# Up projection of a two-layer decoder trunk: high and low halves of the activations taken in one 512-column product

## The chip, the cores and the metric

The kernel runs on 1 core of one Trainium2 chip. The metric is the device time of one execution in microseconds, the median of several runs. Engines are named as in the profile: PE (TensorE, with PEld for its weight loads), DVE (VectorE), ACT (ScalarE), POOL (GpSimd) and SP (SyncE, which here only issues loads).

## The reference, cut to what matters

Two layers run one after the other on 256 rows of 1024 channels. Each has a mixer (two attention branches, gates, an output projection), a feed-forward part with a causal convolution, and a gated embedding. The change lies in the feed-forward part:

```python
def conv_ffn(u, w_up, conv_w, conv_b, w_down):      # u (1, 256, 1024), w_up (1024, 5632)
    up = u @ w_up
    pad = jnp.pad(up, ((0, 0), (CONV_W - 1, 0), (0, 0)))            # CONV_W = 3
    conv = conv_b + sum(pad[:, j:j + length] * conv_w[j] for j in range(CONV_W))
    gate, val = jnp.split(conv, 2, axis=-1)         # 2816 channels each
    return (jax.nn.gelu(gate, approximate=True) * val) @ w_down
```

All inputs and the output are float32.

## The kernel before, in words

**Three products for one.** A float32 product a·w is made of three products in PE's float32r format. Each operand is split into a high part (rounded to that format) and a low part (what the rounding left), and hi·hi + lo·hi + hi·lo are added up in PSUM.

**Weights.** All weights come as 128 chunks of 128x1024 per layer, in the order of use. `dma_next` (L146) issues a chunk's load on SP into one of 5 `raw` buffers. `split_hi` (L154) makes its high part `wh` on ACT (L159), `split_lo` (L163) its low part `wl` on DVE (L166); after it the next load is issued into the raw buffer that this frees. `chunk` (L195) hands a pair to the products. `tick` (L200), called between pieces of work, goes on with the splitting. In the steady part of the up projection the tick behind chunk n issues the low part of chunk n+4 and then the high part of chunk n+5, so a high part is made one chunk before its low part is asked for, and a low part is issued three chunks before PE reaches it. There are 7 `wh` and 7 `wl` buffers.

**Order.** The order of each engine's instructions is the order in which the program issues them: every engine works through its own queue in order. `Side` (L60) keeps a rough account of the engines' time and decides where side threads (attention pieces, transposes) are put between the products.

**Activations.** `HL` (L271) holds a transposed activation as high tiles and low tiles of 4 k-blocks each, one k-block being 128 channels by 256 rows. `split_T2` (L284) and `ffn_T` (L761) fill it from transposes in PSUM: ACT writes the high part, DVE the low part.

**Up projection (L793 to L825).** A layer has 44 chunks (54 to 97): for each of 22 blocks of 128 channels one chunk of the gate half and one of the value half. For one chunk PE makes 24 products of 256 columns into half of a PSUM bank: for each of 8 k-blocks wh with u's high part (L802), wh with u's low part (L803), wl with u's high part (L804). Then ACT scales the result by the convolution's last tap and adds the bias (L807), and DVE adds the two shifted taps (L809, twice). After each pair ACT makes the gelu (L815) and DVE the product of the halves (L816); the split of that product for the next stage (L821 on ACT, L822 on DVE) is a side thread. Four PSUM banks (`tp`) are used in turn. The down projection (L847) follows, with 22 chunks and 264 products of 512 columns.

**POOL** does small row statistics (L248, L249, L263 to L265) and nothing in the up projection.

Of the kernel before, what the change touches and what calls it, by code (L numbers as in the profile page):

```python
# [9 lines left out]
F32 = mybir.dt.float32  # L10
# [7 lines left out]
P = 128  # L18
# [35 lines left out]
MID_0 = 2  # L54
MID_M = 2
MID_P = 2
NONE = (0.0, 0.0, 0.0)


# [49 lines left out]
def decoder_kernel(ctx: ExitStack, tc: tile.TileContext, x, pT, ws, fc, tb, gf, rope, out):  # L109
# [36 lines left out]
    def dma_next(step=CW):  # L146
# [4 lines left out]
        raws[nx["dma"]] = raw  # L151
        nx["dma"] += 1

    def split_hi():  # L154
        raw = raws[nx["hi"]]
        wh = wpool.tile([P, CW], F32R, name="wh", bufs=SPLITS)
        wl = wpool.tile([P, CW], F32R, name="wl", bufs=SPLITS)
        parts[nx["hi"]] = (wh, wl)
        nc.scalar.activation(wh, raw, AF.Copy)  # L159
        side.work(act=0.95)  # L160
        nx["hi"] += 1

    def split_lo():  # L163
        raw = raws.pop(nx["lo"])
        wh, wl = parts[nx["lo"]]
        nc.vector.tensor_sub(wl, raw, wh.bitcast(F32))  # L166
        side.work(dve=1.12)
        nx["lo"] += 1
        if nx["dma"] < NALL:
            dma_next()  # L170
# [100 lines left out]
    class HL:  # L271


        def __init__(self, name, n=2):
            self.h = [b4(name + "h", F32R) for _ in range(n)]
            self.l = [b4(name + "l", F32R) for _ in range(n)]

        def hi(self, k):
            return self.h[k // 4][:, k % 4, :]

        def lo(self, k):
            return self.l[k // 4][:, k % 4, :]

    def split_T2(srcs, hf, k0, scale, x, between=None):  # L284


        hi, lo = x.h[hf][:, k0:k0 + 2, :], x.l[hf][:, k0:k0 + 2, :]
        n = 1 if callable(scale) else 2
        pts = []
        for a in range(0, 2, n):  # L290
            pt = ps_tp.tile([P, 2, L], F32, name="tp")[:, :n, :]
            pts.append(pt)
            for j in range(n):
                for i in range(2):
                    c = (k0 + a + j) * P
                    nc.tensor.transpose(pt[:, j, i * P:(i + 1) * P], srcs[i][:, c:c + P], ident)  # L296
        for a in range(0, 2, n):
            s = scale if n == 2 else scale(4 * hf + k0 + a)
            nc.scalar.activation(hi[:, a:a + n, :], pts[a], AF.Copy, scale=s)
            nc.vector.scalar_tensor_tensor(lo[:, a:a + n, :], pts[a], s, hi[:, a:a + n, :].bitcast(F32),  # L300
                                           op0=ALU.mult, op1=ALU.subtract)
            if between:
                between(a)
# [119 lines left out]
    for l in range(DEPTH):  # L423
# [238 lines left out]
        def mixer_a(hq, i):  # L662
            while not {"qa", "mask"} <= flags:
                yield NONE
            pe, sums = maps("qa", product_a, i, hq, mask[i])
            yield 0.9 + 0.9 * i, 0.8 + 0.6 * i, MA + MB * i
            rcp = sm.tile([P, 2, 2], F32, name="rcp", bufs=4)
            nc.vector.reciprocal(rcp, sums)
            for hh in range(4):
                nc.vector.tensor_scalar(pe[:, hh, :], pe[:, hh, :], rcp[:, hh % 2, hh // 2:hh // 2 + 1], None,  # L670
                                        op0=ALU.mult)
            yield 0.0, 0.9 + 0.3 * i, 0.0
            pt = ptrans(pe, 4, i)
            yield 0.5 + 0.5 * i, 0.0, 0.5 + 0.5 * i
            nb = i + 1
            ptv = pt[:, :4 * nb, :].rearrange("p (m r s) t -> p m r s t", r=2, s=nb)
            po = ps_tp.tile([P, 2, L], F32, name="tp")[:, 0, :].rearrange("p (m t) -> p m t", t=P)
            for sb in range(nb):
                for r in range(2):
                    nc.tensor.matmul(po[r * 64:(r + 1) * 64], va[:, sb, :], ptv[:, :, r, sb, :],  # L680
                                     start=sb == 0, stop=sb == i)
            x = o_parts()
            hi, lo = (t[0][:, 2 * hq:2 * hq + 2, i * P:(i + 1) * P] for t in (x.h, x.l))
            nc.scalar.activation(hi, po, AF.Copy)
            nc.vector.tensor_sub(lo, po, hi.bitcast(F32))
            yield 0.85 * nb, 0.4, 0.35
            flags.add(("a", hq, i))
# [54 lines left out]
            gemm_a(o["x"], range(4), stream(l, C_BR + 4 + 2 * hf), 512, ev_a)  # L742
        side.until(lambda: "m0" in flags)
        ss = new_ss()
        pxs = HL("px", 1)
        u = HL("u")
        gb = blk.tile([P, D], F32, tag="blk", name="gb")
        nc.scalar.dma_start(gb, gf[l])
# [12 lines left out]
        def ffn_T(i, hf):  # L761
            pt = ps_tp.tile([P, 4, P], F32, name="tp")
            for k in range(4):
                nc.tensor.transpose(pt[:, k, :], un[i][:, hf, k * P:(k + 1) * P], ident)
            hi, lo = (t[hf][:, :, i * P:(i + 1) * P] for t in (u.h, u.l))
            nc.scalar.activation(hi, pt, AF.Copy)
            nc.vector.tensor_sub(lo, pt, hi.bitcast(F32))

        for hf in range(2):
            def ev(i, acc):  # L770
                nc.vector.tensor_add(h[:, i, HALF[hf]], h[:, i, HALF[hf]], acc)

            def mid_m():
                split_T(msrc[1], 1, 0.5, m)
            if hf:
                nc.scalar.activation(pxs.h[0][:, 0:2, :], px, AF.Copy)
                nc.vector.tensor_sub(pxs.l[0][:, 0:2, :], px, pxs.h[0][:, 0:2, :].bitcast(F32))
                gemm_a(m, range(KD), stream(l, C_OUT + 4), 512, ev_n, {13: lambda: ffn_T(0, 0)}, outer=KD)
            else:
                gemm_a(m, range(KD), stream(l, C_OUT), 512, ev, {MID_M: mid_m})  # L780
                sq_half(ss, 0)
# [9 lines left out]


        gx = []  # L793
        for fb in range(NF):
            cc = []
            for s in range(2):
                wh, wl = chunk(l, C_UP + 2 * fb + s)
                wh = wh.rearrange("p (k f) -> p k f", f=P)
                wl = wl.rearrange("p (k f) -> p k f", f=P)
                pu = ps_tp.tile([P, 512], F32, name="tp")[:, :L]  # L800
                for k in range(KD):
                    nc.tensor.matmul(pu, wh[:, k, :], u.hi(k), start=k == 0, stop=False)  # L802
                    nc.tensor.matmul(pu, wh[:, k, :], u.lo(k), start=False, stop=False)  # L803
                    nc.tensor.matmul(pu, wl[:, k, :], u.hi(k), start=False, stop=k == KD - 1)  # L804
                c = sm.tile([P, L], F32, name="cv", **T2)
                w = cw[:, s * NF + fb, :]
                nc.scalar.activation(c, pu, AF.Identity, bias=w[:, 3:4], scale=w[:, 2:3])  # L807
                for sh in (1, 2):
                    nc.vector.scalar_tensor_tensor(c[:, sh:], pu[:, :L - sh], w[:, 2 - sh:3 - sh], c[:, sh:],  # L809
                                                   op0=ALU.mult, op1=ALU.add)  # L810
                cc.append(c)
                side.work(pe=2.6)
                side.work(dve=0.8, act=0.8)
                tick()
            nc.scalar.activation(cc[0], cc[0], AF.Gelu_apprx_tanh)  # L815
            nc.vector.tensor_mul(cc[1], cc[1], cc[0])  # L816
            if fb % 4 == 0:
                gx.append(HL("g", 1))

            def parts_g(c=cc[1], ghi=gx[-1].hi(fb % 4), glo=gx[-1].lo(fb % 4)):  # L820
                nc.scalar.activation(ghi, c, AF.Copy)  # L821
                nc.vector.tensor_sub(glo, c, ghi.bitcast(F32))  # L822
                yield 0.0, 0.35, 0.3
            side.spawn(parts_g(), 0)
        tick()  # L825


# [19 lines left out]
        for hf in range(2):  # L847
            acc = [ps_acc.tile([P, 512], F32, name="acc") for _ in range(2)]
            for k in range(NF):
                c, r = divmod(hf * NF + k, 2)  # L850
                wh, wl = wdn(c)
                wh, wl = wh[:, r * 512:(r + 1) * 512], wl[:, r * 512:(r + 1) * 512]
                for i in range(2):
                    a = gx[k // 4].hi(k % 4)[:, i * P:(i + 1) * P]
                    b = gx[k // 4].lo(k % 4)[:, i * P:(i + 1) * P]
                    nc.tensor.matmul(acc[i], a, wh, start=k == 0, stop=False)  # L856
                    nc.tensor.matmul(acc[i], a, wl, start=False, stop=False)  # L857
                    nc.tensor.matmul(acc[i], b, wh, start=False, stop=k == NF - 1)  # L858
                side.pe += 1.3
                if k % 2:  # L860
                    tick()
            for i in range(2):
                nc.vector.tensor_add(h[:, i, HALF[hf]], h[:, i, HALF[hf]], acc[i])
            if hf == 0:
                u = HL("u")
                side.spawn(down_side(u))
# [130 lines left out]
```

## Time and profile before

| | |
|---|---|
| median of 3 runs | 799.1 us (797.64 to 799.3) |
| the profiled execution's own time | 798.24 us |
| its span | 796.4 us |
| PE busy | 787.5 us (99%), 4753 products |
| DVE busy | 602.3 us (76%) |
| ACT busy | 474.5 us (60%) |
| POOL busy | 64.2 us (8%) |
| up projection, layer 0 and layer 1 | 189.02 to 315.80 us and 580.90 to 707.70 us |

The span is the time from the first to the last instruction that the profile shows; 1.84 us of the execution's own time lie around it. PE's products are pipelined: the start of one product to the start of the next is what one costs, and the duration given for each is longer than that.

### The profile page before, as it was taken

To read this page: it belongs to the slowest core of one execution; us is meant where nothing else is said; L and a number is where in the kernel's file an instruction comes from. 1 tells how busy PE (TensorE), PEld (TensorE's weight loads), DVE (VectorE), ACT (ScalarE), POOL (GpSimd) and SP (SyncE) were. 2 spreads that over 40 slices of the span, in tenths; PEclk is the share of its full clock that TensorE was granted. 3 is DMA by queue.
4 is the path that set the end of the run, shared out by engine and by line. 5 is a ranking of instruction groups with operands and counts; after the bars stand their busy time and mean duration, and the time that the engine had idled before them with its cause. 6 is when DMAs were issued, how large, how long until landed. Compare 5 with 4: busy or idle time off the path is not lost.

```text
span 796.4 us, 12717 instructions
## 1 busy us (share of the span) xinstructions
PE 787.5 (99%) x4753; PEld 684.6 (86%) x4753; DVE 602.3 (76%) x1078; ACT 474.5 (60%) x835; POOL 64.2 (8%) x86
## 2 busy tenths in 40 slices
PE   8999999999999999999999999999999999999997
PEld 6877877788999999888888778778799999998887
DVE  6987987777888888754687889768688888884643
ACT  6766657456666666543576486664476666663541
POOL 0240300010000000000023213000100000000000
PEclk9999999999999999999999999999999999999999
DMA  8654363464555555656465434445555555557421
GB/s 324 207 176 142 131 193 126 149 232 136 184 186 186 185 186 178 229 172 228 133 194 175 132 134 159 159 135 200 181 165 182 186 184 186 186 194 255 168 98 53
DMA packets 40333, 139.56 MB, mean 175 GB/s; under 512 B 4560, under 2 KB 5968, under 8 KB 40272
## 3 DMA queue, kind: packets, MB, share of 16 engines
q1 hardware_dynamic: 39408, 136.91, 51.8%
q10 hardware_dynamic: 864, 1.84, 0.7%
q8 instruction: 37, 0.61, 0.3%
q14 instruction: 24, 0.20, 0.1%
HBM read 137.69 MB, written 1.05 MB: 174 GB/s over the span
## 4 chain that ended last, share of the span: by engine, by line
PE 90%; DVE 3%; ACT 3%; POOL 1%; issue 1%; DMA 1%; SPq 0%; DVEq 0%; ACTq 0%; POOLq 0%
PE acc L333 12%; PE acc L335 12%; PE acc L334 12%; PE tp L803 11%; PE tp L804 11%; PE tp L802 11%; PE acc L856 5%; PE acc L858 5%; PE acc L857 5%; ACT pe L586 2%; PE tp L296 2%; DVE wl L166 1%; PE tp L601 1%; PE tp L680 1%; PE tp L637 1%
## 5 line engine op out<-in xcount | busy, mean ns | idle before, releaser
L166 DVE TENSOR_TENSOR wl<-raw,wh 128x1024 fp32r<-128x1024 f32 x254 | 306.3, 1219 | 27.3 <-ACT wh L159 27.1
L159 ACT ACTIVATE wh<-raw 128x1024 fp32r<-128x1024 f32 x254 | 264.4, 1058 | 38.9 <-PE acc L858 27.4
L803 PE MATMUL tp<-ul,wh 128*128 128x256 f32 x704 | 199.4, 283 | 0.0
L802 PE MATMUL tp<-uh,wh 128*128 128x256 f32 x704 | 199.4, 283 | 0.0
L804 PE MATMUL tp<-uh,wl 128*128 128x256 f32 x704 | 199.2, 283 | 0.0
L803 PEld LDWEIGHTS tp<-ul,wh 128*128 128x128 f32 x704 | 135.1, 192 | 0.1
L802 PEld LDWEIGHTS tp<-uh,wh 128*128 128x128 f32 x704 | 135.1, 192 | 0.0
L804 PEld LDWEIGHTS tp<-uh,wl 128*128 128x128 f32 x704 | 135.1, 192 | 0.0
L333 PE MATMUL acc<-wh,uh 128*128 128x512 f32 (+1 forms) x336 | 133.8, 398 | 0.0
L335 PE MATMUL acc<-wh,ul 128*128 128x512 f32 (+1 forms) x336 | 130.5, 388 | 0.0
L334 PE MATMUL acc<-wl,uh 128*128 128x512 f32 (+1 forms) x336 | 130.4, 388 | 0.0
L809 DVE SCALAR_TENSOR_TENSOR cv<-tp,fc,cv 128x255 f32<-128x255 f32 (+1 forms) x176 | 84.9, 483 | 40.1 <-ACT cv L807 36.9
L807 ACT ACTIVATE cv<-tp,fc 128x256 f32<-128x256 f32 x88 | 49.8, 566 | 89.9 <-PE tp L804 89.9
L333 PEld LDWEIGHTS acc<-wh,uh 128*128 128x128 f32 x336 | 63.1, 188 | 13.2 <-issue 0.7
L335 PEld LDWEIGHTS acc<-wh,ul 128*128 128x128 f32 x336 | 63.1, 188 | 12.9
L334 PEld LDWEIGHTS acc<-wl,uh 128*128 128x128 f32 x336 | 63.2, 188 | 11.6 <-DVE wl L166 0.2
L856 PE MATMUL acc<-wh,gh 128*128 128x512 f32 x176 | 68.9, 391 | 0.0
L858 PE MATMUL acc<-wh,gl 128*128 128x512 f32 x176 | 68.5, 389 | 0.0
L857 PE MATMUL acc<-wl,gh 128*128 128x512 f32 x176 | 68.5, 389 | 0.0
L263 POOL TENSOR_SCALAR sst<-ss 128x2 f32<-128x2 f32 (+1 forms) x8 | 5.6, 700 | 508.7 <-ACT junk L255 508.5
L586 ACT ACTIVATE pe<-tp,nb,rq 128x256 f32<-128x256 f32 (+1 forms) x64 | 31.8, 526 | 18.0 <-DVE nb L583 12.2
L858 PEld LDWEIGHTS acc<-wh,gl 128*128 128x128 f32 x176 | 33.0, 188 | 6.9
(178 smaller groups left out, 997.9 us busy)
## 6 DMA issues: line engine op xcount, KB each, us to landing
raw<-ws SPq DMA_DIRECT2D x254, 512.0 KB, 3.4
raw<-ws SPq DMA_DIRECT2D x4, 256.0 KB, 5.1
gb<-gf ACTq DMA_DIRECT2D x2, 512.0 KB, 4.3
h<-x SPq DMA_DIRECT2D x2, 256.0 KB, 4.1
h<-x SPq DMA_DIRECT2D x1, 512.0 KB, 6.5
px<-pT ACTq DMA_DIRECT2D x2, 256.0 KB, 2.6
out<-h SPq DMA_DIRECT2D x2, 256.0 KB, 2.0
out<-h SPq DMA_DIRECT2D x4, 128.0 KB, 1.8
```

What stands on the lines that cost most here:

```text
L159: nc.scalar.activation(wh, raw, AF.Copy)
L166: nc.vector.tensor_sub(wl, raw, wh.bitcast(F32))
L333: nc.tensor.matmul(o, a, wh, start=q == 0, stop=False)
L334: nc.tensor.matmul(o, a, wl, start=False, stop=False)
L335: nc.tensor.matmul(o, b, wh, start=False, stop=q == nk - 1)
L802: nc.tensor.matmul(pu, wh[:, k, :], u.hi(k), start=k == 0, stop=False)
L803: nc.tensor.matmul(pu, wh[:, k, :], u.lo(k), start=False, stop=False)
L804: nc.tensor.matmul(pu, wl[:, k, :], u.hi(k), start=False, stop=k == KD - 1)
L809: nc.vector.scalar_tensor_tensor(c[:, sh:], pu[:, :L - sh], w[:, 2 - sh:3 - sh], c[:, sh:], op0=ALU.mult, op1=ALU.add)
L856: nc.tensor.matmul(acc[i], a, wh, start=k == 0, stop=False)
L857: nc.tensor.matmul(acc[i], a, wl, start=False, stop=False)
L858: nc.tensor.matmul(acc[i], b, wh, start=False, stop=k == NF - 1)
```

## The change

- `HL` keeps high and low part of a k-block side by side (k-block, part, row), so that both can be the moving operand of one product of 512 columns (`pair`). Tiles hold 2 k-blocks instead of 4 of one part. `split_T2`, the attention output, `ffn_T` (now two pieces of 2 k-blocks) and the embedding's input write into the new layout.
- A chunk of the up projection takes 8 products of 512 columns (wh with the pair) and 8 of 256 (wl with the high part). The lo·wh sums come out in the second half of the PSUM bank. ACT copies that half to SBUF (`cl`), and DVE adds it to the first half in PSUM; only then come the scaling and the taps.
- The four steps behind a pair of chunks (gelu, product, high part, low part) are put into the next two chunks' sequence, one on ACT between `cl` and the scaling, one on DVE between the addition and the taps.
- In the up projection the low parts of its chunks 6 to 43 are made on POOL, two of every three (26 per layer); the third stays on DVE.

```diff
+POOL_0 = 6
+    def on_pool(c):
+        return C_UP + POOL_0 <= c < C_DN and (c - C_UP) % 3 != 2
...
     def split_lo():
         raw = raws.pop(nx["lo"])
         wh, wl = parts[nx["lo"]]
-        nc.vector.tensor_sub(wl, raw, wh.bitcast(F32))
-        side.work(dve=1.12)
+        if on_pool(nx["lo"] % NCHUNK):
+            nc.gpsimd.tensor_tensor(wl, raw, wh.bitcast(F32), op=ALU.subtract)
+        else:
+            nc.vector.tensor_sub(wl, raw, wh.bitcast(F32))
+            side.work(dve=1.12)
...
-            self.h = [b4(name + "h", F32R) for _ in range(n)]
-            self.l = [b4(name + "l", F32R) for _ in range(n)]
+            self.t = [b4(name, F32R).rearrange("p (k a) t -> p k a t", a=2) for _ in range(n // 2)]
...
+        def pair(self, k):
+            return self.t[k // 2][:, k % 2, :, :]
...
-            hi, lo = (t[hf][:, :, i * P:(i + 1) * P] for t in (u.h, u.l))
-            nc.scalar.activation(hi, pt, AF.Copy)
-            nc.vector.tensor_sub(lo, pt, hi.bitcast(F32))
+            for k in (0, 2):
+                hi, lo = u.two(4 * hf + k, slice(i * P, (i + 1) * P))
+                nc.scalar.activation(hi, pt[:, k:k + 2, :], AF.Copy)
+                nc.vector.tensor_sub(lo, pt[:, k:k + 2, :], hi.bitcast(F32))
...
+        def products(c):
+            wh, wl = (t.rearrange("p (k f) -> p k f", f=P) for t in chunk(l, c))
+            acc = ps_tp.tile([P, 2, L], F32, name="tp")
+            for k in range(KD):
+                nc.tensor.matmul(acc, wh[:, k, :], u.pair(k), start=k == 0, stop=False)
+                nc.tensor.matmul(acc[:, 0, :], wl[:, k, :], u.hi(k), start=False, stop=k == KD - 1)
+            return acc
+
+        def convolved(acc, w, act_too, dve_too):
+            pu = acc[:, 0, :]
+            cl = sm.tile([P, L], F32, name="cl", bufs=3)
+            c = sm.tile([P, L], F32, name="cv", **T2)
+            nc.scalar.activation(cl, acc[:, 1, :], AF.Copy)
+            act_too()
+            nc.vector.tensor_add(pu, pu, cl)
+            nc.scalar.activation(c, pu, AF.Identity, bias=w[:, 3:4], scale=w[:, 2:3])
+            dve_too()
+            for sh in (1, 2):
+                nc.vector.scalar_tensor_tensor(c[:, sh:], pu[:, :L - sh], w[:, 2 - sh:3 - sh], c[:, sh:],
+                                               op0=ALU.mult, op1=ALU.add)
...
+        def gated(cc, gx_):
+            g0_, g1 = cc
+            hi, lo = gx_
+            yield lambda: nc.scalar.activation(g0_, g0_, AF.Gelu_apprx_tanh)
+            yield lambda: nc.vector.tensor_mul(g1, g1, g0_)
+            yield lambda: nc.scalar.activation(hi, g1, AF.Copy)
+            yield lambda: nc.vector.tensor_sub(lo, g1, hi.bitcast(F32))
+
+        steps = [lambda: None] * 4
         for fb in range(NF):
             cc = []
             for s in range(2):
...
+                acc = products(C_UP + 2 * fb + s)
+                cc.append(convolved(acc, cw[:, s * NF + fb, :], steps[2 * s], steps[2 * s + 1]))
                 tick()
...
+            steps = list(gated(cc, (gx[-1].hi(fb % 2), gx[-1].lo(fb % 2))))
+        for f in steps:
+            f()
```

## Rows read from the trace of the kernel before

**Rows 1.** The chain that ended last, shares of the span by engine and line.
```profile
PE 90%; DVE 3%; ACT 3%; POOL 1%; issue 1%; DMA 1%; SPq 0%; DVEq 0%; ACTq 0%; POOLq 0%
PE acc L333 12%; PE acc L335 12%; PE acc L334 12%; PE tp L803 11%; PE tp L804 11%; PE tp L802 11%; PE acc L856 5%; PE acc L858 5%; PE acc L857 5%; ACT pe L586 2%; PE tp L296 2%; DVE wl L166 1%; PE tp L601 1%; PE tp L680 1%; PE tp L637 1%
```
**Rows 2.** Busy us by stretch (instructions), granted clock, DMA share: both up projections.
```profile
core 0: us, PE busy (x) PEld busy (x) DVE busy (x) ACT busy (x) POOL busy (x), PEclk, DMA share, GB/s
189.02:315.80 126.78, 126.78 (x1058) 126.71 (x1057) 106.14 (x174) 81.83 (x133) 0.00 (x0) 1.00 0.57 186
...
580.90:707.70 126.80, 126.80 (x1059) 126.72 (x1057) 106.08 (x174) 81.84 (x133) 0.00 (x0) 1.00 0.57 186
```
**Rows 3.** Waits, 189 to 316 us: who for whom, us, times, longest.
```profile
ACT cv L807 <- PE tp L804: 43.9, 42, 1.4
DVE cv L809 <- ACT cv L807: 18.0, 42, 1.1
```
**Rows 4.** PE's 512-column products in time: start, duration; two stretches.
```profile
182.81 0.40 PE L335 MATMUL acc<-wh,pxl 128*128 128x512 f32 x1
...
184.89 0.39 PE L335 MATMUL acc<-wh,pxl 128*128 128x512 f32 x1
...
329.79 0.39 PE L857 MATMUL acc<-wl,gh 128*128 128x512 f32 x1
...
335.91 0.39 PE L857 MATMUL acc<-wl,gh 128*128 128x512 f32 x1
```
**Rows 5.** Groups by line: busy us, mean ns; idle before, releaser.
```profile
L159 ACT ACTIVATE wh<-raw 128x1024 fp32r<-128x1024 f32 x254 | 264.4, 1058 | 38.9 <-PE acc L858 27.4 <-DMA raw<-ws 10.3 <-DVE wl L166 1.0
...
L809 DVE SCALAR_TENSOR_TENSOR cv<-tp,fc,cv 128x255 f32<-128x255 f32 (+1 forms) x176 | 84.9, 483 | 40.1 <-ACT cv L807 36.9
...
L807 ACT ACTIVATE cv<-tp,fc 128x256 f32<-128x256 f32 x88 | 49.8, 566 | 89.9 <-PE tp L804 89.9
...
L816 DVE TENSOR_TENSOR cv<-cv 128x256 f32<-128x256 f32 x44 | 18.4, 419 | 1.1 <-ACT cv L815 1.1
...
L815 ACT ACTIVATE cv<-cv 128x256 f32<-128x256 f32 x44 | 17.9, 406 | 0.0
...
L767 DVE TENSOR_TENSOR ul<-tp,uh 128x512 fp32r<-128x512 f32 x8 | 5.3, 685 | 1.0 <-ACT uh L766 1.0
...
L766 ACT ACTIVATE uh<-tp 128x512 fp32r<-128x512 f32 x8 | 4.8, 594 | 6.7 <-PE tp L764 6.7
...
L685 DVE TENSOR_TENSOR ol<-tp,oh 128x256 fp32r<-128x256 f32 x8 | 3.4, 425 | 11.7 <-ACT oh L684 11.7
...
L684 ACT ACTIVATE oh<-tp 128x256 fp32r<-128x256 f32 x8 | 3.1, 384 | 11.9 <-PE tp L680 11.8
```
**Rows 6.** The same view for POOL, and one line's min/median/max ns.
```profile
L236 POOL MEMSET cm<- 128x256 f32 x1 | 0.3, 312 | 0.0
...
masks.py:197 POOL MEMSET ident<- 128x128 f32 x1 | 0.2, 205 | 0.3 <-POOLq L986 0.3
...
L264 POOL TENSOR_TENSOR sst<-sst,ss x8: 191/303/945, 21.9 to 774.8; 128x2 f32<-128x2 f32 x4, 128x1 f32<-128x1 f32 x4
```
**Rows 7.** DVE and POOL in order of time: start us, us, where they meet.
```profile
88.79 1.22 DVE L166 TENSOR_TENSOR wl<-raw,wh 128x1024 fp32r<-128x1024 f32 x1
...
88.96 1.10 POOL L248 TENSOR_SCALAR pw<-hss 128x8 f32<-128x8 f32 x1 [6.46 <-DVE hss L396]
...
80.59 0.20 POOL L248 TENSOR_SCALAR pw<-hss 128x8 f32<-128x8 f32 x1 [19.99 <-DVE rcp L623]
...
52.03 0.69 DVE L390 TENSOR_TENSOR qr<-m,m 128x512 f32<-128x512 f32 x1
...
51.45 1.69 POOL L249 TENSOR_TENSOR rq<-pw,mhalf 128x8 f32<-128x8 f32 x1
```
**Rows 8.** DVE's low parts: durations min/median/max in ns.
```profile
L166 DVE TENSOR_TENSOR wl<-raw,wh x254: 1211/1218/1237, 12.7 to 783.5; 128x1024 fp32r<-128x1024 f32 x127
```
**Rows 9.** DMA issues: KB each, median us to landing.
```profile
raw<-ws SPq DMA_DIRECT2D x254, 512.0 KB, 3.4
```

More of the change, by code (lines that the diff above doesn't have):

```diff
@@ L271, in decoder_kernel, with __init__, two @@
     class HL:
-        def __init__(self, name, n=2):
-            self.h = [b4(name + "h", F32R) for _ in range(n)]
-            self.l = [b4(name + "l", F32R) for _ in range(n)]
+        def __init__(self, name, n=KD):
+            self.t = [b4(name, F32R).rearrange("p (k a) t -> p k a t", a=2) for _ in range(n // 2)]
         def hi(self, k):
-            return self.h[k // 4][:, k % 4, :]
+            return self.t[k // 2][:, k % 2, 0, :]
         def lo(self, k):
-            return self.l[k // 4][:, k % 4, :]
+            return self.t[k // 2][:, k % 2, 1, :]
+        def pair(self, k):
+            return self.t[k // 2][:, k % 2, :, :]
+        def two(self, k, cols=slice(0, L)):
+            return (self.t[k // 2][:, :, a, cols] for a in range(2))
     def split_T2(srcs, hf, k0, scale, x, between=None):
-        hi, lo = x.h[hf][:, k0:k0 + 2, :], x.l[hf][:, k0:k0 + 2, :]
+        hi, lo = x.two(4 * hf + k0)
         n = 1 if callable(scale) else 2
@@ L682, in mixer_a @@
             x = o_parts()
-            hi, lo = (t[0][:, 2 * hq:2 * hq + 2, i * P:(i + 1) * P] for t in (x.h, x.l))
+            hi, lo = x.two(2 * hq, slice(i * P, (i + 1) * P))
             nc.scalar.activation(hi, po, AF.Copy)
@@ L744, in decoder_kernel @@
         ss = new_ss()
-        pxs = HL("px", 1)
+        pxs = HL("px", 2)
         u = HL("u")
@@ L775, in decoder_kernel @@
             if hf:
-                nc.scalar.activation(pxs.h[0][:, 0:2, :], px, AF.Copy)
-                nc.vector.tensor_sub(pxs.l[0][:, 0:2, :], px, pxs.h[0][:, 0:2, :].bitcast(F32))
+                pxh, pxl = pxs.two(0)
+                nc.scalar.activation(pxh, px, AF.Copy)
+                nc.vector.tensor_sub(pxl, px, pxh.bitcast(F32))
                 gemm_a(m, range(KD), stream(l, C_OUT + 4), 512, ev_n, {13: lambda: ffn_T(0, 0)}, outer=KD)
@@ L793, in decoder_kernel @@
         gx = []
+        def products(c):
[17 more added lines that the diff above has]
+                                               op0=ALU.mult, op1=ALU.add)
+            side.work(pe=2.5)
+            side.work(dve=1.8, act=1.3)
+            return c
+        def gated(cc, gx_):
[6 more added lines that the diff above has]
+        steps = [lambda: None] * 4
         for fb in range(NF):
@@ L796, in decoder_kernel @@
             for s in range(2):
[L797 to L813, printed above, removed]
-                tick()
[L815 to L824, printed above, removed]
+                acc = products(C_UP + 2 * fb + s)
+                cc.append(convolved(acc, cw[:, s * NF + fb, :], steps[2 * s], steps[2 * s + 1]))
+                tick()
+            if fb % 2 == 0:
+                gx.append(HL("g", 2))
+            steps = list(gated(cc, (gx[-1].hi(fb % 2), gx[-1].lo(fb % 2))))
+        for f in steps:
+            f()
         tick()
@@ L853, in decoder_kernel @@
                 for i in range(2):
-                    a = gx[k // 4].hi(k % 4)[:, i * P:(i + 1) * P]
-                    b = gx[k // 4].lo(k % 4)[:, i * P:(i + 1) * P]
+                    a = gx[k // 2].hi(k % 2)[:, i * P:(i + 1) * P]
+                    b = gx[k // 2].lo(k % 2)[:, i * P:(i + 1) * P]
                     nc.tensor.matmul(acc[i], a, wh, start=k == 0, stop=False)
```

## The prediction

> **What bounds the kernel now.** I read the chain of waits first. 90% of it is PE, and the three product lines of the up projection (L802 to L804) are 33 points of that [rows 1]. Then the table by stretch: in both up projections PE is busy for the whole stretch, at a granted clock of 1.00, its 2.4 GHz level [rows 2]. Then the waits inside the first of them: ACT waits 43.9 us for PE and DVE 18.0 us for ACT, and PE stands in no row as the one that waits [rows 3]. So the up projection lasts as long as PE issues products, DVE has 126.78 - 106.14 = 20.6 us of room per layer and ACT 126.78 - 81.83 = 45.0 us. A change there is worth what it takes from PE's issue, as long as the others stay inside PE's shorter time.
>
> **PE: the gain.** 44 chunks x 24 = 1056 products took 126.78 us [rows 2], 0.1201 us each, 2.881 us per chunk. A product of 512 columns costs, from start to start, (335.91 - 329.79) / 27 = 0.2267 us in the steady part of the down projection [rows 4]. Twice the columns cost 0.1066 us more, so a product carries 0.0135 us that don't grow with its columns. A chunk now takes 8 x (0.2267 + 0.1201) = 2.774 us: the columns stay at 6144, the products fall from 24 to 16. That is 0.107 us per chunk, 88 x 0.107 = **9.4 us**. The worst 512-column spacing I find, between products with other work around them, is (184.89 - 182.81) / 9 = 0.2311 us [rows 4]; by it a chunk costs 2.810 us and the gain is 6.3 us. No stretch shows a shorter spacing than 0.2267, so I leave no room for more than 9.4, and take 9.4 because the up projection is as steady as the stretch that it comes from. PE stays without gaps, so nothing asks for another clock.
>
> **What is added on ACT.** `cl`, 256 columns out of PSUM: 0.384 us, as L684 does the same; the slower form with scale and bias takes 0.566 [rows 5]. ACT's work per layer becomes 81.8 + 44 x 0.384 = 98.7 us (106.7 at most) in 44 x 2.774 = 122.1. In order, with full durations: `cl` 0.38, then it waits for DVE's addition (0.42) and puts a gate step of 0.41 there, scaling 0.57, a high part 1.06 [rows 5]: 0.38 + 0.42 + 0.57 + 1.06 = 2.43 us of 2.774, and 2.61 with the dear `cl`. ACT holds. If DVE is late with the addition, the scaling and the next high part behind it are late too.
>
> **What is added on DVE, and what goes.** The addition reads and writes PSUM, which no row does. Nearest are L685 (PSUM in, SBUF out) at 0.425 and the tap at 0.483 [rows 5]; I take 0.42. 26 low parts of 1.218 us per layer go [rows 8]: 106.1 + 44 x 0.42 - 26 x 1.22 = 92.9 us of 122.1. In order, a chunk costs DVE addition 0.42, the wait for the scaling 0.57 (a gate step of 0.42 lies in it), two taps 0.97: 1.96 us, and 3.18 with a low part. Over a group of three that is 7.10 us against PE's 8.32. The low parts are issued three chunks before PE needs them and four PSUM banks go round, so DVE may be 3 x 2.774 - 3.56 (`cl` and a full chunk) = 4.8 us late before PE sees it. The first two chunks of the stretch and its last four, behind which DVE still makes low parts, lose 0.41 us each, at most 1.6 us in a row: hidden. Without this cover each would cost its 0.41.
>
> **POOL's low parts.** No row shows an operation of this size on POOL. Two memsets give 0.107 us per 128 elements [rows 6], 0.84 ns an element; the small TENSOR_TENSOR takes 0.19 us at least. With one pass 1024 elements make 0.19 + 0.86 = 1.05 us, with two passes for two inputs 1.9, with a third for the output 2.8. I take 1.9. POOL has two per group of 8.32 us, so any price up to 4.16 us fits by itself, and POOL's queue holds nothing else in the stretch [rows 2]. SP issues the next load behind each low part and now waits for POOL there, with all later loads queued behind it. That load lands in 3.4 us [rows 9] and its high part is made four chunks (11 us) after the low part was issued: hidden up to 7 us of delay.
> The Trainium skill, GPSIMD Engine Reference, section "Elementwise — side-by-side cycle accounting", gives 4497 ns for a two-input addition of 2048 elements; my estimate from it is 2.25 us for 1024. That would change nothing in the sum. No run here shows it yet.
>
> **POOL and DVE in each other's way.** An operation of 0.20 us on POOL took 1.10 when it began under a low part on DVE, and ended at 90.06, 0.05 us after it (88.79 + 1.22) [rows 7]: POOL waits for DVE. The other way round the trace shows nothing: L390, with two inputs in SBUF, ran 52.03 to 52.72 inside POOL's L249 (51.45 to 53.14) in its usual 0.69 us [rows 7], and of 254 low parts none took over 1.237 us [rows 8]. But those POOL operations touch 8 columns. I take it that POOL gives way: two operations of 1.9 us and waits for three gate steps and one low part, at most 3.8 + 2.48 = 6.3 of 8.32 us.
> The Trainium skill says otherwise: SBUF — State Buffer, section "Who interferes with whom", has a DVE instruction with two SBUF inputs and a POOL instruction that reads SBUF exclude each other, the first to issue keeping the ports for its whole length. The trace agrees for POOL behind DVE; L390 speaks against the whole length the other way. What it would make here are the first two rivals below.
>
> **Small terms.** `ffn_T` makes two pieces of 256 per k-block pair instead of one of 512: at most 2 x 0.384 - 0.594 = 0.17 us on ACT and 2 x 0.42 - 0.685 = 0.16 on DVE [rows 5]; only the last of the four per layer is near PE, and its first piece comes sooner than before. -0.2 to +0.3 us per layer, taken as 0.15. The new layout moves addresses, not counts.
>
> **Sum.** 798.24 - 9.4 + 0.3 = 789.1 us against the profiled execution's own time (span 796.4 and 1.84 around it). The median of the runs lies 0.86 us above that execution: **790.0 us**.
>
> **The rivals.**
> *POOL keeps DVE out, and gets in first.* A gate step (two SBUF inputs) stands ahead of the taps in every chunk, so if it waits for a whole POOL operation, everything behind it on DVE waits, then the scaling on ACT, then the high part. Follow a group with DVE late and 1.9 us on POOL, which starts when a high part ends: the third chunk's low part waits for POOL, 1.95 to 3.85 us, and ends at 5.07; the next addition 5.49; gate step, taps to 7.03 while POOL starts at 7.1; the next addition 7.45, its gate step held to 9.0, taps to 10.39. A group takes 10.4 us, 3.46 per chunk, 0.69 over PE. For 38 chunks that is 26 us, less the 4.8 of room: 21 per layer, 790 + 42 = **832 us**. It breaks even with before at groups of about 9.1 us. For it: POOL's visible waiting, and that a high part ends just where DVE comes to its low part. Against: L390.
> *The same, but DVE's low part gets in first.* Then only the two gate steps are held: low part to 3.18, POOL to 5.08, gate step to 5.50, taps to 6.47; POOL again to 7.40, gate step 7.82, taps 8.79. 2.93 per chunk, 38 x 0.156 = 5.9 less 4.8: 1 us per layer, 792 us. Each 0.1 us more on POOL adds 0.2 to the group, so 2.05 us on POOL is break-even and 2.2 gives about 808. I put this case at **797 us**.
> *The change doesn't do what it says on PE.* A 512-column product followed by a 256-column one could cost the 0.360 us of three small ones, if the loading of weights sets the pace rather than the columns. Then nothing is gained: **799 us**. For it: PEld is busy throughout the stretch too, 126.71 us [rows 2]. Against: the 512-column products load weights of the same size, and their 0.2267 us is less than two of 0.1201.
>
> **Chances and range.** Forecast 0.60; POOL first 0.18; DVE first 0.15 (0.09 faster, 0.03 same, 0.03 slower); no gain on PE 0.07 (0.02, 0.04, 0.01). A measurement of this kernel can tell about 0.2% (1.6 us). Faster 0.60 + 0.09 + 0.02 = 0.71, same 0.07, slower 0.18 + 0.03 + 0.01 = 0.22. The forecast's own range is 788.5 to 793.5, its end the 0.2311 spacing. Taking in the case without a gain and DVE-first up to nearly 808 gives 788 to 806; POOL-first and the dear end of DVE-first stay out, 2 in 10.
>
> **What would show it.** Right: the up projections last about 122.1 us each, products start every 0.227 and 0.120 us in turn, DVE's rows and gate steps keep 0.42 and 1.22 us, ACT still waits for PE, and PE for nobody. POOL rows of 1.9 us, up to 3 where they meet DVE. Wrong: products of the up projection that wait for a low part or for the taps; gate steps on DVE that last, or start late by, the length of a POOL operation; PE's spacing above 0.347 per pair without a wait.

## The result, and the profile after

The changed kernel takes **814.3 us** (median; 813.1 to 814.6) against 799.2 for the kernel before in the same runs: a ratio of 1.018 [1.017, 1.020]. The forecast was 790.0 us, with a range up to 806; the change made the kernel slower, by 1.8%. The profiled execution took 814.1 us, its span 812.3.

The page's chain of waits, shares by engine, answers to [rows 1]:

```profile
PE 53%; DVE 32%; ACT 8%; issue 5%; POOL 1%; DMA 1%; SPq 0%; DVEq 0%; ACTq 0%; POOLq 0%
```

PE had 90% of the chain and has 53%; DVE came from 3% to 32%. Next the two up projections by stretch, from their first product to their last, with the columns of [rows 2]:

```profile
189.16:319.41 130.25, 126.08 (x708) 107.74 (x706) 121.26 (x183) 92.37 (x174) 77.33 (x26) 1.00 0.48 173
592.67:722.87 130.20, 126.35 (x707) 107.77 (x705) 121.20 (x183) 92.39 (x174) 77.28 (x26) 1.00 0.48 173
```

Read, like these, up to the next stage's first product (before: 315.94 and 707.92), they last 3.3 and 3.2 us longer than before instead of some 4.9 us less. DVE has 26 low parts fewer and is nevertheless busy for 121.2 us instead of 106.1; the forecast's 92.9 misses 28 us of that. PE is busy for 126.1 us, 4 us less than the stretch, and its granted clock is 1.00 throughout. The waits of the first stretch (compare [rows 3]: who for whom, us, times, longest):

```profile
ACT cv L829 <- DVE tp L828: 33.7, 40, 1.4
...
PE tp L816 <- DVE cv L832: 3.1, 8, 0.4
```

ACT waited for PE; now it waits for DVE, and PE itself waits for DVE eight times. The groups by line (busy us, mean ns; idle before, releaser) name the instructions that grew, compare [rows 5, 8]:

```profile
L174 DVE TENSOR_TENSOR wl<-raw,wh 128x1024 fp32r<-128x1024 f32 x202 | 243.1, 1220 | 22.6 <-ACT wh L164 22.0
...
L172 POOL TENSOR_TENSOR wl<-raw,wh 128x1024 fp32r<-128x1024 f32 x52 | 154.6, 2994 | 105.8 <-ACT wh L164 99.5
...
L832 DVE SCALAR_TENSOR_TENSOR cv<-tp,fc,cv 128x255 f32<-128x255 f32 (+1 forms) x176 | 84.3, 479 | 15.6 <-ACT cv L829 12.4
...
L843 DVE TENSOR_TENSOR cv<-cv 128x256 f32<-128x256 f32 x44 | 55.1, 1252 | 0.9 <-ACT cv L842 0.9
L845 DVE TENSOR_TENSOR g<-cv,g 128x256 fp32r<-128x256 f32 x44 | 54.4, 1237 | 1.0 <-ACT g L844 1.0
```

The taps and DVE's low parts are as they were. The two gate steps on DVE, L843 (the product of the halves) and L845 (its low part), take 1.25 and 1.24 us where the product took 0.419 before. Beside the low parts, they alone have two inputs in SBUF in these stretches. Over 44 of each that is 44 x (1.252 + 1.237 - 0.84) = 73 us, 36 per layer. The stretch shows 28 of it because DVE leaves work behind: 183 of its instructions lie in it, and 174 + 44 - 26 = 192 were due.

One group of three chunks in time (start, duration), first POOL, then DVE:

```profile
236.14 5.95 POOL L172 TENSOR_TENSOR wl<-raw,wh 128x1024 fp32r<-128x1024 f32 x2 [3.16 <-ACT wh L164]
245.25 5.95 POOL L172 TENSOR_TENSOR wl<-raw,wh 128x1024 fp32r<-128x1024 f32 x2 [3.16 <-ACT wh L164]
```
```profile
236.07 1.22 DVE L174 TENSOR_TENSOR wl<-raw,wh 128x1024 fp32r<-128x1024 f32 x1
237.20 0.42 DVE L828 TENSOR_TENSOR tp<-tp,cl 128x256 f32<-128x256 f32 x1
237.54 2.30 DVE L843 TENSOR_TENSOR cv<-cv 128x256 f32<-128x256 f32 x1
239.76 0.99 DVE L832 SCALAR_TENSOR_TENSOR cv<-tp,fc,cv 128x255 f32<-128x255 f32 x2
240.66 0.42 DVE L828 TENSOR_TENSOR tp<-tp,cl 128x256 f32<-128x256 f32 x1
241.00 1.38 DVE L845 TENSOR_TENSOR g<-cv,g 128x256 fp32r<-128x256 f32 x1
242.30 0.99 DVE L832 SCALAR_TENSOR_TENSOR cv<-tp,fc,cv 128x255 f32<-128x255 f32 x2
243.20 0.42 DVE L828 TENSOR_TENSOR tp<-tp,cl 128x256 f32<-128x256 f32 x1
243.53 0.41 DVE L843 TENSOR_TENSOR cv<-cv 128x256 f32<-128x256 f32 x1
244.26 1.00 DVE L832 SCALAR_TENSOR_TENSOR cv<-tp,fc,cv 128x255 f32<-128x255 f32 x2 [0.31 <-ACT cv L829]
```

DVE's low part starts at 236.07, POOL's pair of operations at 236.14. Alone, two such operations take 2 x 2.40 = 4.80 us (measured below); the pair's other 1.15 us is the time until the low part ends at 237.29, for which POOL is held. Then the gate step issued at 237.54 lasts 2.30 us, 1.88 more than usual; the next is held for 0.96; the third meets no POOL and takes 0.41. The addition at 240.66 and the taps, which read PSUM, keep their lengths (0.42, and 0.99 for the two taps) while POOL runs. A duration in this view thus includes time in which the instruction only stood. The group takes 245.25 - 236.14 = 9.11 us where PE needs 8.32. PE feels it from 250.00 on, and then once in each group (start, duration, idle before, releaser):

```profile
250.00 0.47 PE L816 MATMUL tp<-u,wh 128*128 128x512 f32 x1 [0.39 <-DVE cv L832]
```

Outside the up projections the down projection of the first layer takes 67.6 us instead of 60.6, from the start of its first product to that of its last, and here is most of that (start, duration, idle before, releaser):

```profile
335.87 0.50 PE L891 MATMUL acc<-wl,g 128*128 128x512 f32 x1 [4.29 <-DVE wl L174]
...
336.81 0.63 PE L891 MATMUL acc<-wl,g 128*128 128x512 f32 x1
337.24 0.63 PE L892 MATMUL acc<-wh,g 128*128 128x512 f32 x1
```

PE stands for 4.29 us, and then eight products start 0.43 us apart instead of 0.23: the granted clock from 336.40 to 339.90 is 0.51, PE's level of 1.2 GHz instead of 2.4, which costs another 1.6 us. The low part that it waits for stood behind this DVE instruction, which waits for a table (after, then before):

```profile
328.88 0.33 ACTq L865 DMA_DIRECT2D tbl<-tb  x1
...
332.70 0.29 DVE L375 TENSOR_TENSOR rt_ka<-rp,tbl 128x128 f32<-128x128 f32 x1 [2.95 <-DMA tbl<-tb]
```
```profile
319.25 0.34 ACTq L831 DMA_DIRECT2D tbl<-tb  x1
...
323.01 0.29 DVE L361 TENSOR_TENSOR rt_ka<-rp,tbl 128x128 f32<-128x128 f32 x1 [2.90 <-DMA tbl<-tb]
```

DVE waited 2.90 us for it before too, and PE never saw it. Then the table was asked for 3.3 us after the end of the up projection (at 315.94), now 9.5 us after it (at 319.41): DVE's lateness is handed on to the next stage, and the old wait comes on top.

At the start of each up projection a smaller stall appears, first on ACT and then on PE:

```profile
191.86 0.38 ACT L781 ACTIVATE u<-tp 128x256 fp32r<-128x256 f32 x1 [0.49 <-DVE u L782]
```
```profile
191.88 0.51 PE L816 MATMUL tp<-u,wh 128*128 128x512 f32 x1 [1.07 <-DVE u L782]
```

`ffn_T` now makes two pieces, and ACT's second piece waits for DVE's low part of the first; the tile of PSUM that both read is all that the two share. PE's own wait is 1.07 us, but its first chunk costs more: 4.40 us instead of 2.77 in the first layer, 4.42 in the second, as some products around the wait start late too.

### The profile page after: what moved, and what is told of

Same layout as the page of the kernel before. It is cut to its first block, busy times and chain, and to the rows that moved or that the text cites. A ratio compares the mean times of both kernels' runs of the same rounds, so it can differ in the third digit from the quotient of the medians.

```text
span 812.3 us, 11570 instructions
## 1 busy us (share of the span) xinstructions
PE 789.2 (97%) x4049; PEld 647.0 (80%) x4049; DVE 641.7 (79%) x1122; ACT 500.8 (62%) x931; POOL 219.9 (27%) x138
## 3 DMA queue, kind: packets, MB, share of 16 engines
HBM read 137.69 MB, written 1.05 MB: 171 GB/s over the span
## 4 chain that ended last, share of the span: by engine, by line
PE 53%; DVE 32%; ACT 8%; issue 5%; POOL 1%; DMA 1%; SPq 0%; DVEq 0%; ACTq 0%; POOLq 0%
PE acc L347 11%; PE acc L349 11%; PE acc L348 11%; DVE cv L832 8%; DVE cv L843 6%; DVE g L845 5%; DVE wl L174 5%; PE acc L891 4%; PE acc L892 4%; PE acc L890 4%; DVE tp L828 3%; ACT cv L829 2%; ACT pe L600 2%; PE tp L310 1%; PE tp L615 1%
## 5 line engine op out<-in xcount | busy, mean ns | idle before, releaser
L816 PE MATMUL tp<-u,wh 128*128 128x512 f32 x704 | 250.4, 399 | 8.0 <-DVE cv L832 5.8
L817 PE MATMUL tp<-u,wl 128*128 128x256 f32 x704 | 197.5, 280 | 0.0
L172 POOL TENSOR_TENSOR wl<-raw,wh 128x1024 fp32r<-128x1024 f32 x52 | 154.6, 2994 | 105.8 <-ACT wh L164 99.5
L816 PEld LDWEIGHTS tp<-u,wh 128*128 128x128 f32 x704 | 132.1, 188 | 44.8 <-ACT g L844 5.3
L347 PE MATMUL acc<-wh,u 128*128 128x512 f32 (+1 forms) x336 | 133.8, 398 | 0.0
L817 PEld LDWEIGHTS tp<-u,wl 128*128 128x128 f32 x704 | 133.0, 189 | 0.0
L349 PE MATMUL acc<-wh,u 128*128 128x512 f32 (+1 forms) x336 | 130.5, 389 | 0.0
L348 PE MATMUL acc<-wl,u 128*128 128x512 f32 (+1 forms) x336 | 130.4, 388 | 0.0
L891 PE MATMUL acc<-wl,g 128*128 128x512 f32 x176 | 70.0, 398 | 4.6 <-DVE wl L174 4.3
L347 PEld LDWEIGHTS acc<-wh,u 128*128 128x128 f32 x336 | 63.1, 188 | 13.2 <-issue 0.7
L349 PEld LDWEIGHTS acc<-wh,u 128*128 128x128 f32 x336 | 63.1, 188 | 12.9
L890 PE MATMUL acc<-wh,g 128*128 128x512 f32 x176 | 69.6, 395 | 0.0
L892 PE MATMUL acc<-wh,g 128*128 128x512 f32 x176 | 69.2, 393 | 0.0
L843 DVE TENSOR_TENSOR cv<-cv 128x256 f32<-128x256 f32 x44 | 55.1, 1252 | 0.9 <-ACT cv L842 0.9
L845 DVE TENSOR_TENSOR g<-cv,g 128x256 fp32r<-128x256 f32 x44 | 54.4, 1237 | 1.0 <-ACT g L844 1.0
```

The lines of the kernel that those rows point to most:

```text
L172: nc.gpsimd.tensor_tensor(wl, raw, wh.bitcast(F32), op=ALU.subtract)
L347: nc.tensor.matmul(o, a, wh, start=q == 0, stop=False)
L348: nc.tensor.matmul(o, a, wl, start=False, stop=False)
L349: nc.tensor.matmul(o, b, wh, start=False, stop=q == nk - 1)
L816: nc.tensor.matmul(acc, wh[:, k, :], u.pair(k), start=k == 0, stop=False)
L817: nc.tensor.matmul(acc[:, 0, :], wl[:, k, :], u.hi(k), start=False, stop=k == KD - 1)
```

## The experiments

Every ratio is against the kernel before on the same chip. Theory 1 is that POOL's low part, while it reads, holds every DVE instruction with two SBUF inputs, and that everything queued on DVE behind a held gate step is late with it. Its rivals are that DVE or ACT has too much work in any case, and that the two stalls, at the table and at the start of the up projection, make the difference.

**gate_psum.** The gate steps work in PSUM, in the second half of the value chunk's bank, which is free once `cl` is copied out; counts and order stay (excerpt; the gelu now writes to `ps` too):

```
-yield lambda: nc.vector.tensor_mul(g1, g1, g0_)
+yield lambda: nc.vector.tensor_mul(ps, ps, g1)      # ps = acc[:, 1, :]
...
-yield lambda: nc.vector.tensor_sub(lo, g1, hi.bitcast(F32))
+yield lambda: nc.vector.tensor_sub(lo, ps, hi.bitcast(F32))
```

> The gelu is written into the unused second half of the PSUM bank of the value chunk, the product of the halves is made there in place, and the high and low part are taken from there: each gate step on DVE reads one operand in SBUF and one in PSUM instead of two in SBUF. Nothing else changes; the result is the same. Theory 1 (a POOL low part and a DVE instruction with two SBUF operands exclude each other for their whole length): the gate steps return from 1.25 us to 0.42, a group of three chunks from 9.1 to about 8.3 us, each up projection from 130.2 to 123 to 125 us (1.1 us of start loss stay), and with DVE no longer late the 4.3 us wait in layer 0's down projection goes too: 793 to 798 us in all. Theory 2 (DVE is too long by its own added work and by the to and fro with ACT; the long gate steps only show it): the up projections stay above 128 us, 808 us or more in all.

Measured: 797.1 us, ratio 0.998 [0.996, 0.999]. The two groups by line:

```profile
L843 DVE TENSOR_TENSOR tp<-tp,cv 128x256 f32<-128x256 f32 x44 | 18.6, 423 | 0.9 <-ACT tp L842 0.9
L845 DVE TENSOR_TENSOR g<-tp,g 128x256 fp32r<-128x256 f32 x44 | 18.2, 414 | 0.9 <-ACT g L844 0.9
```

One operand moved to PSUM gives the 0.42 us back, with as many operations on POOL as before, and takes 2.0% off the time. Theory 1 holds; the work that the forecast gave DVE, 93 us per layer, fits. The stall at the start is still in this run, and the table is asked for as before, so neither made the difference.

**pool_memset.** POOL writes `wl` twice and reads nothing, so the low weights' products of these chunks are left out of the result.

```
-nc.gpsimd.tensor_tensor(wl, raw, wh.bitcast(F32), op=ALU.subtract)
+nc.gpsimd.memset(wl.bitcast(F32), 0.0)
+nc.gpsimd.memset(wl.bitcast(F32), 0.0)
```

> POOL fills the low parts it is given with zeros, in two fills of 1024 columns, instead of subtracting: it writes the same tile for about the same time (2 x 1.05 us by the memsets' slope) but reads nothing from SBUF. The hi x lo products of 52 chunks are thereby left out of the result. Theory 1: if it is POOL's reading that keeps DVE out, the gate steps return to 0.42 us and the up projections to 123 to 125 us, 793 to 798 us in all. If writing alone keeps DVE out, gate steps stay above 1 us and the time at 810 or more. Theory 2: no change from 814.

Measured: 797.2 us, 0.998 [0.996, 1.000].

```profile
L172 POOL MEMSET wl<- 128x1024 f32 x52 | 49.7, 956 | 121.4 <-PE tp L818 113.1 <-PE acc L349 8.3
...
L844 DVE TENSOR_TENSOR cv<-cv 128x256 f32<-128x256 f32 x44 | 18.3, 416 | 1.0 <-ACT cv L843 1.0
```
```profile
243.02 0.95 POOL L173 MEMSET wl<- 128x1024 f32 x1
...
243.09 0.41 DVE L846 TENSOR_TENSOR g<-cv,g 128x256 fp32r<-128x256 f32 x1
```

POOL is busy for 1.9 us per low part and the gate steps, still with both inputs in SBUF, take 0.416, also where one lies wholly inside a memset, as at 243.09. POOL's writing doesn't hold DVE, so far as a memset stands for it; what is left is its reading.

**no_pool.** DVE makes all low parts.

```
-POOL_0 = 6
+POOL_0 = 44
```

> All low parts stay on DVE; products, convolution and gate steps as in the changed kernel. Theory 1: without POOL a chunk costs DVE what the last four of the up projection show, 3.11 us (319.10 to 322.21 to 325.31), against 3.03 with POOL: about 0.08 x 38 = 3 us more per layer, 818 to 826 us in all; gate steps 0.42. Rival (POOL's part is what loses; without it the rest pays): 805 us or less.

Measured: 813.2 us, 1.019 [1.018, 1.021]; below the 818 to 826 that were expected, and about the same as with POOL. Two chunks of the later part of a stretch, the first stretch, and the table's work on DVE behind it:

```profile
293.20 1.22 DVE L174 TENSOR_TENSOR wl<-raw,wh 128x1024 fp32r<-128x1024 f32 x1
...
295.39 1.00 DVE L832 SCALAR_TENSOR_TENSOR cv<-tp,fc,cv 128x255 f32<-128x255 f32 x2 [0.31 <-ACT cv L829]
296.31 1.22 DVE L174 TENSOR_TENSOR wl<-raw,wh 128x1024 fp32r<-128x1024 f32 x1
```
```profile
189.23:322.00 132.77, 130.95 (x708) 107.72 (x706) 115.94 (x208) 91.67 (x174) 0.00 (x0) 1.00 0.51 169
```
```profile
357.92 0.28 DVE L375 TENSOR_TENSOR rt_ka<-rp,tbl 128x128 f32<-128x128 f32 x1
```

DVE without help needs 3.11 us a chunk, 9.33 a group; with POOL's help 9.11. POOL takes two low parts of 1.22 us off a group, holding the gate steps gives 1.88 + 0.96 = 2.84 us back, and the wait of 0.31 us for ACT's scaling comes once a group instead of once a chunk: 9.33 - 2.44 + 2.84 - 0.62 = 9.11.

So each up projection takes 132.8 us, 2.5 longer than with POOL, much as expected. What the expectation missed is the stage behind the first one. `split_lo` adds to `Side`'s account of DVE's work (`side.work(dve=1.12)`) only where DVE makes the low part, so the edit changed this account too, and with it the places of the side threads: the table's work came at 357.92 instead of 332.70 and waited for nothing, and the down projection took 62.1 us instead of 67.6. The equal totals of the two kernels are the sum of two differences, and no measure of POOL's help.

**ffn_order.** In `ffn_T` both high parts are issued ahead of both low parts (shortened):

```
-for k in (0, 2): hi, lo; activation(hi); tensor_sub(lo)
+for k in (0, 2): activation(hi)
+for k in (0, 2): tensor_sub(lo)
```

> In the feed-forward transposes both high pieces are issued before both low pieces, so that ACT's second piece no longer waits for DVE's first. Expected by the trace of the changed kernel: the wait of 1.1 us of the first chunk of each up projection for u's low part goes, 812 us (-2.2). Rival: DVE is the bound in that stretch anyway and only waits elsewhere: 814, no change.

Measured: 810.9 us, 1.016 [1.014, 1.017]: 3.4 us less where some 2 were expected. The wait at the start is gone, and the first chunk of the two stretches takes 2.94 and 2.95 us instead of 4.40 and 4.42: the stall cost 1.5 us per layer, 2.9 in all, and not only PE's wait of 1.1. The half microsecond that is left is within the scatter of the runs.

**table_early.** The table's load is issued ahead of the up projection instead of in the down projection.

```
+if l + 1 < DEPTH:                                   # ahead of the up projection
+    tbl = sm.tile([P, 512], F32, name="tbl", bufs=1)
+    nc.scalar.dma_start(tbl, tb[l + 1])
...
-tbl = sm.tile([P, 512], F32, name="tbl", **T2)      # in the down projection
-nc.scalar.dma_start(tbl, tb[l + 1])
```

> The changed kernel, with the load of the next layer's table issued ahead of the up projection instead of behind it; the work on the table stays where it was. In layer 0 of the changed kernel DVE stands 2.95 us at that load, which ACT issued late, and PE then 4.3 us at the low part queued behind the table work, after which eight products run at half the clock. Theory (the delay that DVE and ACT have gathered in the up projection is only handed on to the down projection): the wait in DVE goes, PE's wait falls below 1 us, the clock stays: 807 to 810 us. Rival (PE would wait for the late low parts anyway): 813 or more. The up projections stay at 130 us by both.

Measured: 809.5 us, 1.014 [1.012, 1.015], a time as expected. PE's wait in the down projection is not below 1 us, though:

```profile
332.71 0.50 PE L892 MATMUL acc<-wl,g 128*128 128x512 f32 x1 [1.25 <-DVE wl L174]
```

1.25 instead of 4.29, and the products behind it start 0.23 us apart: 3.0 + 1.6 us, nearly all of the 4.8 by which the two profiled executions differ.

**gate_psum_pool_all.** As gate_psum, and POOL makes all low parts from the 7th chunk on (without the condition `and (c - C_UP) % 3 != 2`).

> As gate_psum, and POOL makes all low parts of chunks 6 to 43 of the up projection, so that DVE has no instruction with two SBUF operands left there. Theory 1: POOL's subtractions run undisturbed and show their own length, about 2.3 us (the pair in gate_psum took 4.64 us after the DVE low part had let go), 2.4 of 2.8 us a chunk at most, and PE stays the bound: the same 794 to 799 us as gate_psum. Rival (POOL becomes the bound, or its lateness reaches PE): up projections above 127 us, 800 or more.

Measured: 797.5 us, 0.999 [0.997, 1.000]; no gain over gate_psum. With DVE out of its way POOL shows the price of its own operation (min/median/max ns), a term of the prediction that no row had shown:

```profile
L172 POOL TENSOR_TENSOR wl<-raw,wh x76: 2397/2406/3420, 201.6 to 695.6; 128x1024 fp32r<-128x1024 f32 x76
```

**all_mended** is gate_psum, ffn_order and table_early together; **all_mended_pool_all** has all low parts on POOL besides.

> gate_psum with ffn_order and table_early. If the three losses are separate, they add up: 797.1 (gate_psum) - 2.4 (the start of both up projections) - 0.8 (the wait left in layer 0's down projection) = 793.9, with runs between 791.5 and 796.5, since a whole up projection runs at 2.774 or at 2.827 us per chunk. If they overlap: 796 or more.

> all_mended with all low parts of chunks 6 to 43 on POOL. By theory 1 the same as all_mended, 791.5 to 796.5: DVE has room in both. Should DVE's remaining low parts, which still wait behind POOL, cost something, it is faster by that; a POOL that falls behind would make it 797 or more.

Measured: 790.8 us, 0.990 [0.989, 0.992], and 790.7 us, 0.990 [0.989, 0.992]. Both up projections of all_mended, and what is left of PE's and ACT's waits in the first:

```profile
189.40:311.67 122.27, 122.27 (x707) 107.73 (x706) 92.25 (x189) 96.07 (x176) 75.33 (x26) 1.00 0.53 191
576.70:698.93 122.23, 122.23 (x707) 107.69 (x706) 92.24 (x189) 96.04 (x176) 75.40 (x26) 1.00 0.52 189
```
```profile
ACT cv L833 <- DVE tp L832: 15.4, 42, 0.9
...
ACT u L781 <- PE tp L778: 0.6, 1, 0.6
```

PE is busy for the whole 122.2 us and waits for nobody. Both times lie just below the 791.5 to 796.5 that were expected, as all four up projections ran at the better of the two paces that the last section shows. This version beats both kernels, by 1.0% and 2.8%.

**gate_behind_taps.** The gate steps stay in SBUF, but `dve_too()`, which issues DVE's, is moved behind the loop of the taps, so that a held step should delay less (shortened).

```
-dve_too()
 for sh in (1, 2):
     nc.vector.scalar_tensor_tensor(...)
+dve_too()
```

> The changed kernel with DVE's gate step put behind the two taps instead of ahead of them; operands as in the changed kernel, two in SBUF. Theory 1: POOL still holds the step until its reading ends, but the taps (one SBUF operand, one in PSUM) now run meanwhile, so less of the hold is left when the step comes: by the rows of the changed kernel a group falls from 9.1 to about 8.8 us, gate steps last 0.6 to 0.9 us instead of 1.25, 804 to 809 us in all. Rival (the step's place fills a wait for ACT, and without it DVE stands 0.3 to 0.6 us more per chunk): 814 or more.

Measured: 849.6 us, 1.064 [1.062, 1.066]. The expectation, 804 to 809, had the wrong sign. POOL, then DVE:

```profile
241.08 2.58 POOL L172 TENSOR_TENSOR wl<-raw,wh 128x1024 fp32r<-128x1024 f32 x1 [2.25 <-ACT wh L164]
...
251.57 2.58 POOL L172 TENSOR_TENSOR wl<-raw,wh 128x1024 fp32r<-128x1024 f32 x1 [2.25 <-ACT wh L164]
```
```profile
241.34 3.40 DVE L174 TENSOR_TENSOR wl<-raw,wh 128x1024 fp32r<-128x1024 f32 x1
244.67 0.42 DVE L828 TENSOR_TENSOR tp<-tp,cl 128x256 f32<-128x256 f32 x1
```

Now POOL issues 0.26 us ahead of DVE's low part instead of 0.07 us behind it. The low part is held and takes 3.40 us, everything of the next chunk is behind it, and the group takes 251.57 - 241.08 = 10.49 us. The mechanism is theory 1's; the expectation took it that DVE's low part would still get in first, and moving the step changed that.

**gate_psum_ffn.** gate_psum and ffn_order without the early table.

> gate_psum with ffn_order, without table_early. It tells the two apart that all_mended has together. Start loss alone, 1.1 us per layer: 797.1 - 2.2 = 794.9. If an up projection that begins without a wait also always runs at 2.774 us per chunk and never at 2.827 (2.3 us per layer, as all six such stretches so far did), then on average about 2.7 us more: 791.5 to 793, with little scatter.

Measured: 790.4 us, 0.991 [0.989, 0.992], the same as all_mended. Once DVE isn't late, loading the table early gains nothing that can be measured, though PE still waits 0.9 us for a low part in that down projection. It lies below gate_psum by 0.7%, more than the 2.9 us of the two starts; what the rest is stands in the last section.

## Why the prediction was wrong

**The step that failed is "I take it that POOL gives way".** POOL does wait for DVE, as [rows 7] showed; DVE waits for POOL as well, and only the first half was counted. The evidence for it was too weak: L390 ran inside a POOL operation at its usual 0.69 us, and the 254 low parts [rows 8] were never held, but the POOL operations beside them moved 8 columns. They could only show that a POOL operation with little to read doesn't hold DVE. The step "DVE's rows and gate steps keep 0.42 and 1.22 us" is wrong for the gate steps (1.25 and 1.24 us on average) and right for the low parts, the addition (0.424) and the taps (0.479). The two runs that removed only the conflict, by an operand in PSUM or by a POOL that doesn't read, came out at 0.998 instead of 1.018.
The Trainium skill, SBUF — State Buffer, section "Who interferes with whom", had stated this exclusion, and the prediction set L390 against it. The trace of after agrees: 2.30 us instead of 0.42 behind POOL, and no delay for the instructions with an operand in PSUM. Whether it is the "whole length" this trace can't settle: POOL, free to go at 237.29, let the gate step end at 239.84, which less its own 0.42 is a hold of 2.13 us; reckoned the same way the second operation, from 239.69 on, held the next step for 2.27; and the operation alone takes 2.40.

**The rival that happened is the second, DVE first, and its price was too low.** Its order of events is the trace's. With 1.9 us on POOL it gave 8.79 us a group; by its own rule, with holds of 2.13 and 2.27 us, it gives 8.79 + 0.23 + 0.37 = 9.39; measured 9.11. But even 9.11, which is 9.11 / 3 - 2.774 = 0.263 us a chunk over PE's time, makes its sum 790 + 2 x (38 x 0.263 - 4.8) = 800 us; most of the other 14 us are in the next two terms. The term for POOL, taken as 1.9 between 1.05 and 2.8, measures 2.40. A number from the nearest rows, memsets of 128 and 256 columns, was no measure for an operation with two inputs. The estimate of 2.25 us from the Trainium skill (GPSIMD Engine Reference, the section named in the prediction) was nearer, 0.16 us short of the 2.406 measured.

The first rival's 10.4 us a group isn't what the change does, but gate_behind_taps shows it with POOL first: 10.49. In the change DVE was ahead by 0.07 us.

**The term "4.8 us late before PE sees it"** treats that room as free. DVE uses it up, and from 250.00 on eight groups lose 9.11 - 8.32 = 0.79 us each, 6.3 us in the first layer; with the 1.6 us of the first chunk that is 7.9 of the 8.2 by which the stretch misses the forecast. What is in the room is not hidden but handed on: when PE had ended the up projection, DVE still owed it, the table was asked for 6 us later, and the down projection paid 4.29 us for the wait and 1.6 for PE's lower clock. table_early gets 4.6 of the down projection's 7.0 us back (63.0 us). In the second layer there is no table to load, and the down projection is only 0.9 us longer than before.

**The small term for `ffn_T`, "-0.2 to +0.3 us per layer",** counted durations and no wait: ACT's second piece stands behind DVE's first. That costs 1.5 us per layer by ffn_order, and some of the stretches that begin so run at a worse pace of PE (last section).

**PE's step is right**, though not in every stretch. The first layer of after keeps 2.77 us per chunk until DVE is late, and all_mended keeps it to the end: 122.27 us against 44 x 2.774 = 122.06, and 790.8 us against 790.0. The third rival, no gain on PE, is out. But the second layer of after runs at 2.83 from its second chunk on, 0.353 us a pair without a wait, which the prediction had named as a sign of being wrong. It cost nothing there, as DVE set the length: 130.2 us in both layers. **ACT's step is right** too: it never set the pace; its waits are for DVE. **DVE's own work was priced right**: 3.18 us for a chunk with a low part against 3.11 in no_pool, 92.9 us per layer against 92.25 in all_mended. What went wrong was the price of running it beside POOL.

The gap between forecast and result, in ratios to before: forecast 0.989; gate_psum_ffn 0.991; gate_psum 0.998; after 1.018. So 2.0 points are the exclusion with what it hands on, 0.7 the start of the up projection with the pace that goes with it, and the rest is within the intervals.

## What to carry to other kernels

Before work is moved to POOL, list the DVE instructions that will run beside it: here those with two inputs in SBUF were held for 2.1 to 2.3 us by each POOL subtraction of 1024 columns. Put one of their operands in PSUM, or don't move the work: until then POOL, with two low parts of three, took only 0.22 us off a group of 9.33. A small operation that passes unharmed is no evidence for a large one. Room that a late engine uses up isn't free: look at what the next stage starts with.

## What the runs showed of the hardware that was not expected

PE runs a whole up projection at one of two paces. In gate_psum the first layer, then the second, five pairs of products each (start, duration):

```profile
229.92 0.40 PE L816 MATMUL tp<-u,wh 128*128 128x512 f32 x1
...
231.68 0.40 PE L816 MATMUL tp<-u,wh 128*128 128x512 f32 x1
...
599.84 0.39 PE L816 MATMUL tp<-u,wh 128*128 128x512 f32 x1
...
601.57 0.40 PE L816 MATMUL tp<-u,wh 128*128 128x512 f32 x1
```

1.76 against 1.73 us; over whole stretches 0.3533 and 0.3467 us a pair, at a granted clock of 1.00 in both. The pace is there from the start and stays as long as PE isn't stopped: 44 x 8 x 0.0066 = 2.3 us per layer, 4.7 for both, which is about the scatter of gate_psum's runs (794.6 to 799.5). Of the fourteen stretches that began with the 1.1 us wait five ran at the better pace and nine at the other, until DVE held PE up; the eight without that wait (ffn_order, gate_psum_ffn and both all_mended kernels) all ran at the better one. That is why gate_psum_ffn lies further below gate_psum than the 2.9 us of the two starts. In ffn_order itself the pace brought nothing: its first layer ran at the better one as after's did, and still came out 1.8 us shorter. What sets the pace, and why the wait matters to it, is open.
